# Grouped-query attention in one core: setup order on GpSimd, early transposes, idle matmuls, and the last period's steps

## The chip, the core and the metric

The kernel runs on one core of a Trainium2 chip. The core has five engines that run side by side, each working through its own list of instructions in order: TensorE (PE, matrix products; its weight loads are listed as PEld), VectorE (DVE), ScalarE (ACT), GpSimd (POOL) and SyncE (SP, which here only issues DMAs). They meet by semaphores. Matrix products are written to PSUM, all other tiles lie in SBUF, and DMA queues move data between SBUF and device memory. The metric is the time of one execution on the device in microseconds (us); lower is better. The kernel before takes 414.74 us, the median of three runs (413.86 to 415.82).

## The reference

Softmax attention with 32 query heads and 8 key/value heads, four query heads to each key/value head:

```python
batch, seq, n_heads, n_kv_heads, dim = 8, 512, 32, 8, 64
scale = 1.0 / np.sqrt(dim)
K_expanded = np.repeat(K, heads_per_group, axis=2)
V_expanded = np.repeat(V, heads_per_group, axis=2)
scores = np.einsum('bhqd,bhkd->bhqk', Q, K_expanded) * scale
weights = np.exp(scores - np.max(scores, axis=-1, keepdims=True))
weights = weights / (np.sum(weights, axis=-1, keepdims=True) + 1e-10)
output = np.einsum('bhqk,bhkd->bhqd', weights, V_expanded)
```

Q is (8, 512, 32, 64), K and V are (8, 512, 8, 64), all float32, as is the output.

## The kernel before

**Units, pairs and tiles.** `fast_path` does all the work. (After it a flag says whether every row sum lay in a safe range, and `general_path` would compute everything anew if not; it does not run here.) Two neighbouring key/value heads of one batch with their eight query heads are a *unit*; there are 32 of them (u = 0 to 31). A unit has four *pairs* of query heads. For one pair and one block of 128 keys (kc = 0 to 3), PE writes a *score tile* of 128 keys by 2 x 512 queries (`scores`, L241, two matmuls), and an exponential turns it into a block of weights `pt`. When a pair's four blocks are there, PE multiplies them with V (`pv`, L304, 32 small matmuls in eight *chunks* of four; chunks 6 and 7 belong to the block that comes last). V carries a column of ones, so that the row sums come out beside the result. DVE takes the reciprocal of the sums (`inverse`, L320) and multiplies (`norm`, L331) into the output tile `o_sb` of the unit. `norm` also stores: a unit's 1 MB goes out in one DMA on SP's queue when the fourth of its pairs is done, except in the very last unit (u = 31), where each pair sends its own 256 KB.

**Two ways to take the exponential.** Most score tiles go to ACT (`exp_act`, L255). Of each eight pairs, five have their last block computed elsewhere (`DVE_KCS`): DVE turns the scores into an integer with the bits of a power of two (U, L266), masks them (F, L271), GpSimd computes a correction in two steps (G, L276, and W, L284), and DVE joins both (P, L288).

**The order by hand.** There are 16 *periods* (n = 0 to 15) of eight pairs, two units each. Nothing reorders instructions: each engine's list follows from the order in which the token list is read, `STEPS` for periods up to 14 and `FINISH` for period 15. A token is a letter and a number: S5 fills the sixth ACT score tile of the period, A5 takes its exponential. V5.1-3 does chunks 1 and 2 of pair 5, R5 and N5 its reciprocal and normalisation. D, U, F, G, W, P with a number are the steps of the period's first to fifth DVE exponential, for pairs 0, 1, 3, 5 and 6 (small g and w do the correction on DVE). T transposes a part of Q on PE (with, once, a check of V), C copies it out on DVE, K and H check V, B gathers the check of the sums, Q and k start loads, E ends the check. "@1" means a step of the period before, "@-1" of the next one; "a", "b" and "s" say which PSUM tile is used: `d_ps` (one buffer), `pv` (one) or `s_ps` (two). As `d_ps` and `pv` are single, a step that needs one waits until DVE has read what was in it. With two score tiles, S may fill its tile as soon as ACT is done with the tile before the last.

In period 0 all of pairs 0 and 1 goes through ACT (the A step of a pair's last tile fills and takes the fourth block too), which makes 434 exponentials on ACT.

**The start** (L497 to L530). SP loads Q heads 0 and 1 (`q_start`) and K heads 0 and 1 in two pieces (`k_start`: the first of four 128-key groups, then three). GpSimd makes the identity for PE's transposes, issues loads of Q heads 2 to 3 and 4 to 7 (`load_q(0, (2, 4, 8))`, L505), then sets constants (L506 to L510), then issues the other loads. DMAs that convert float32 to bf16 are issued by GpSimd. PE meanwhile multiplies a tile of zeros (`spin`, L493). The first Q and K parts are cast on DVE and ACT, transposed on PE and copied by DVE.

**Early transposes.** `EARLY` names what PE must still transpose for unit 0 and the first K heads while the first exponentials run: at key 1 the second Q pair of key/value head 0 (four transposes), at 2 the K head 1 (eight), at 3 the Q pairs of head 1 (eight), at 5 and 6 the K heads 2 and 3 (eight each). They stand behind the A step of that number, and each uses `d_ps` and a DVE copy. In period 0, where a V token of the period before has no work, `spin` issues one idle matmul of 256 columns for each of its chunks (L540).

Of the kernel before, what the change touches and what calls it, by code (L numbers as in the profile page):

```python
# [48 lines left out]
).split()  # L49
FINISH = (  # L50
# [10 lines left out]
).split()  # L61


# [19 lines left out]
def fast_path(ctx, tc, Q, K, V, out, flag):  # L83
    nc = tc.nc
    B, S, H, D = Q.shape
# [43 lines left out]
    def load_k(b, lo=0, hi=KV):  # L129
        if b not in kn:  # L130
            kn[b] = knat_pool.tile([128, SC, KV, D], BF16, name="k_nat")
        nc.gpsimd.dma_start(
            out=kn[b][:, :, lo:hi, :],
            in_=K[b, :, lo:hi, :].rearrange("(p sc) g d -> p sc g d", p=128),
        )
# [7 lines left out]
    def load_q(w, cuts=(0, 4 * HPG)):  # L143
        b, half = divmod(2 * w, GP)
        h0 = half * 2 * HPG
        if w not in qn:
            qn[w] = qnat_pool.tile([128, SC, 4 * HPG, D], BF16, name="q_nat")
        for lo, hi in zip(cuts[:-1], cuts[1:]):
            nc.gpsimd.dma_start(  # L149
                out=qn[w][:, :, lo:hi, :],  # L150
                in_=Q[b, :, h0 + lo:h0 + hi, :].rearrange("(sc p) h d -> p sc h d", p=128),
            )

    def d_tile():
        return d_pool.tile([128, 2, S], FP32, name="d_ps")
# [4 lines left out]
    def s_tile():  # L160
        return s_pool.tile([128, 2, S], FP32, name="s_ps")

    def region(tok):
        return {"a": d_tile, "b": pv_tile, "s": s_tile}[tok[-1]]()

    def first_k(gp, g, bank, lo=0, hi=SC):
        half_bank = bank.bitcast(BF16)[:, 0:S]
        ps = half_bank.rearrange("p (sc c) -> p sc c", sc=SC)
        for sc in range(lo, hi):
            for half in (0, 64):  # L170
                nc.tensor.transpose(ps[half:half + 64, sc, :], kn[0][:, sc, 2 * gp + g, :], ident)  # L171
        keys = slice(lo * 128, hi * 128)
        return lambda: nc.vector.tensor_copy(
            out=kt_first[:, gp, g, keys], in_=half_bank[:, keys]
        )
# [11 lines left out]
    def trans_q(u, g, bank, lo=0, hi=NPAIR):  # L187
        ps = bank.bitcast(BF16).rearrange("p (i sc c) -> p i sc c", i=NPAIR, sc=SC)
        for i in range(lo, hi):
            for sc in range(SC):  # L190
                h = ((u % 2) * 2 + g) * HPG + 2 * i
                nc.tensor.transpose(ps[:, i, sc, :], qn[u // 2][:, sc, h:h + 2, :], ident)  # L192
        if u not in qt:
            qt[u] = qt_pool.tile([128, 2, NPAIR, S], BF16, name="qt")
        return lambda: nc.vector.tensor_copy(  # L195
            out=qt[u][:, g, lo:hi, :], in_=ps[:, lo:hi, :, :].rearrange("p i sc c -> p i (sc c)")
        )
# [10 lines left out]
    def early_q(g, lo):  # L208
        return lambda bank: trans_q(0, g, bank, lo)

    def early_k(gp, g):
        return lambda bank: first_k(gp, g, bank)

    EARLY = {1: [early_q(0, 1)], 2: [early_k(0, 1)], 3: [early_q(1, 0)], 5: [early_k(1, 0)],
             6: [early_k(1, 1)]}

    every = [(p, kc) for p in range(PPAIR) for kc in range(SC)]
    ON_DVE = [(p, kc) for p, kc in every if kc in DVE_KCS[p]]
# [2 lines left out]
    def on_dve(n, k):  # L221
        return n * PPAIR + ON_DVE[k][0] >= NPAIR
# [26 lines left out]
    def fill(p, kc):  # L249
        ps = s_tile()  # L250
        scores(p, kc, ps)
        filled[p, kc] = ps

    def exp_act(p, kc):
        nc.scalar.activation(  # L255
            out=pt_of(p)[:, kc, :, :], in_=filled.pop((p, kc)), func=EXP, scale=scale
        )
# [161 lines left out]
    def step(tok, n):  # L419
        what, k = tok[0], int(tok[1:].split(".")[0].rstrip("ab"))  # L420
        q, kc = ON_DVE[k] if what in "DUFGWPgwsa" else (0, 0)
        if what == "S":
            fill(n * PPAIR + ON_ACT[k][0], ON_ACT[k][1])
            if k == 9 and n == 0:
                dma_k(0, TURNED)
            if k == 2 and n % 2 == 1 and n // 2 + 1 < B:
                dma_k(n // 2 + 1)
        elif what == "A":
            q, kc = ON_ACT[k]
            p = n * PPAIR + q  # L430
            exp_act(p, kc)
            if ON_ACT[k + 1:k + 2] == [] or ON_ACT[k + 1][0] != q:
                for d, (dq, dkc) in enumerate(ON_DVE):
                    if dq == q and not on_dve(n, d):
                        fill(p, dkc)
                        exp_act(p, dkc)
            if n == 0 and k in EARLY:
                bank = d_tile()
                for copy in [turn(bank[:, 1, :]) for turn in EARLY[k]]:
                    copy()  # L440
            if (n, k) == (0, 4):
                second_loads()
        elif what in "VRN":
            p = n * PPAIR + k
            if what == "V":
                lo, hi = tok[3:].rstrip("abs").split("-")
                pv(p, int(lo), int(hi), tok)
            else:
                (inverse if what == "R" else norm)(p)
        elif what in "TKCH":  # L450
            j = n * PPAIR // NPAIR + k
            if j < 2:
                pass
            elif what == "T":
                transposes(j, region(tok))
            elif what == "K":
                check_values(j)
            else:
                read(j if what == "C" else (j, "v"))
        elif what == "Q":  # L460
            loads(n, k)
        elif what == "B":
            if n < NPER - 1:
                bulk_check(n)
        elif what == "E":
            (early_check, verdict)[k]()
        elif what in "sa":
            (fill if what == "s" else exp_act)(n * PPAIR + q, kc)
        elif on_dve(n, k):
            p = n * PPAIR + q  # L470
            if what == "D":
                exp_fill(p, kc, region(tok))
                return
            st = chain.get((p, kc))
            if what == "U":
                exp_bits(st)
            elif what == "F":
                exp_low(st)
            elif what in "Gg":
                slope(nc.gpsimd if what == "G" else nc.vector, st["f"], st["g"])  # L480
            elif what in "Ww":
                bend(nc.gpsimd if what == "W" else nc.vector, st["f"], st["g"], st["w"])
            elif what == "P":
                exp_join(p, kc)
# [3 lines left out]
    def spin(count, columns):  # L488
        if not idle:
            idle.append(pv_tile())  # L490
        bank = idle[0]
        for _ in range(count):
            nc.tensor.matmul(  # L493
                bank[:, 1, 0:columns], warm[:, 0:128], warm[:, 0:columns], start=True, stop=True
            )
# [6 lines left out]
            in_=K[0, :, 0:2, :].rearrange("(p sc) g d -> p sc g d", p=128)[:, lo:hi, :, :],  # L502
        )
    make_identity(nc, ident)
    load_q(0, (2, 4, 8))  # L505
    nc.gpsimd.memset(ones, 1.0)  # L506
    nc.gpsimd.memset(off, 0)
    for j in range(2):
        for c in (0, VW - 1):
            nc.gpsimd.memset(vt[j][:, :, :, c:c + 1], 1.0)  # L510
    load_k(0, 2, 4)
    load_q(0, (8, 16))
    load_v(0, 0, 1)
# [15 lines left out]
    copy = first_k(0, 0, s_tile()[:, 0, :], 1, SC)  # L529
    copy()  # L530

    for period in range(-2, NPER):
        for entry in STEPS if period < NPER - 1 else FINISH:
            tok, _, late = entry.partition("@")
            n = period - int(late or 0)
            if 0 <= n < NPER:
                step(tok, n)
            elif period == 0 and n < 0 and tok[0] == "V":
                lo, hi = tok[3:].rstrip("abs").split("-")
                spin(int(hi) - int(lo), S // 2)  # L540


def general_path(tc, Q, K, V, out):
# [114 lines left out]
```

## Time and profile before

| | us |
|---|---|
| median of three runs (lowest, highest) | 414.74 (413.86, 415.82) |
| the profiled execution, its own time | 415.06 |
| span of the profiled execution | 413.2 |
| ACT busy / PE / DVE / POOL | 400.7 / 380.7 / 334.3 / 276.6 |
| first exponential of a score tile starts | 7.75 |
| last exponential ends | 407.83 |

How to read it. The page is of one execution; "busy" is the time an engine worked, and ends of matmuls are modelled. Lines of the timeline give the start, the duration, engine, line of the kernel, operation, output and input, "xN" for N instructions taken together, and in brackets how long the engine was idle before and what ended that. Equal neighbours are merged, so a line's duration can be that of many. "Landing" is the time from the start of a DMA's issue to its completion. Engines overlap the tail of one instruction with the start of the next, so starts are a better measure of the pace than durations.

### The profile page before, as it was taken

How to read it: one execution, taken by the hardware profiler on the slowest of the kernel's cores; microseconds unless marked ns; L12 is line 12 of the kernel's file. 1: busy time of each engine (PE TensorE's matmuls, PEld its weight loads, DVE VectorE, ACT ScalarE, POOL GpSimd, SP SyncE). 2: the span in 40 equal slices, each digit the busy share in tenths (PEclk: the TensorE clock that was granted, in tenths of full speed). 3: DMA queues.
4: the chain of work that ended last, by engine and by line, in shares of the span. 5: the costliest groups of instructions: out<-in, count | busy, mean ns of one | idle time of the engine just before them, and what ended most of it. 6: DMA issues, size and time to landing. Idle time of an engine off the chain costs nothing.

```text
span 413.2 us, 13322 instructions
## 1 busy us (share of the span) xinstructions
PE 380.7 (92%) x5825; PEld 242.1 (59%) x5825; DVE 334.3 (81%) x617; ACT 400.7 (97%) x438; POOL 276.6 (67%) x208
## 2 busy tenths in 40 slices
PE   8999989899998999989899998999989899998995
PEld 3556656566565655656565565656656565665553
DVE  2488897878889788897878889788797878889885
ACT  4999999999999999999999999999999999999994
POOL 8066776677766677676676766667776677766750
PEclk9999999999999999999999999999999999999998
DMA  9969788687769797589865979849788698652205
GB/s 148 197 123 191 190 157 200 156 165 175 158 169 179 129 215 176 138 192 238 170 122 136 181 168 216 202 105 172 194 158 198 165 167 173 158 161 103 103 37 174
DMA packets 65406, 67.74 MB, mean 164 GB/s; under 512 B 35264, under 2 KB 39872, under 8 KB 65344
## 3 DMA queue, kind: packets, MB, share of 16 engines
q0 software_dynamic: 28128, 24.91, 41.1%
q1 hardware_dynamic: 37216, 41.95, 34.4%
q8 instruction: 46, 0.75, 0.7%
q14 instruction: 16, 0.13, 0.1%
HBM read 50.33 MB, written 33.55 MB: 203 GB/s over the span
## 4 chain that ended last, share of the span: by engine, by line
ACT 76%; PE 20%; DMA 1%; DVE 1%; issue 1%; SPq 0%; ACTq 0%
ACT pt L255 76%; PE s_ps L241 9%; PE pv L304 5%; PE d_ps L304 3%; DMA k_start<-in_K_dram 1%; PE pv L493 1%; PE d_ps L192 1%; DVE pt L288 0%; PE d_ps L171 0%; ACTq L255 0%; DVE o_sb L331 0%; PE s_ps L171 0%; ACT k_nat L524 0%; SPq L500 0%; SPq L498 0%
## 5 line engine op out<-in xcount | busy, mean ns | idle before, releaser
L255 ACT ACTIVATE pt<-s_ps 128x1024 f16<-128x1024 f32 x434 | 398.4, 1283 | 2.8 <-PE s_ps L241 2.8
L304 PEld LDWEIGHTS <-pt 128*128 128x128 f16 x4096 | 142.4, 98 | 65.9 <-issue 55.0
L241 PE MATMUL s_ps<-qt,kt 64*128 64x512 bf16 x810 | 158.8, 383 | 23.1 <-ACT pt L255 20.0
L284 POOL TENSOR_TENSOR w<-g,f 128x1024 bf16<-128x1024 bf16 x77 | 164.1, 2132 | 6.4
L276 POOL TENSOR_SCALAR g<-f 128x1024 bf16<-128x1024 int16 x77 | 80.5, 1045 | 115.7 <-DVE f L271 115.7
L304 PE MATMUL pv<-v,pt 128*128 128x65 bf16 x2560 | 114.8, 195 | 0.2
L241 PEld LDWEIGHTS <-kt 64*128 64x128 bf16 x960 | 57.0, 93 | 65.2 <-issue 34.9
L266 DVE TENSOR_SCALAR u<-d_ps 128x1024 int16<-128x1024 f32 x48 | 58.6, 1221 | 19.8 <-PE d_ps L241 19.8
L304 PE MATMUL d_ps<-v,pt 128*128 128x65 bf16 x1536 | 66.6, 194 | 1.2 <-DVE pt L288 0.9
L331 DVE TENSOR_TENSOR o_sb<-pv,inv 128x512 f32<-128x512 f32 x80 | 55.3, 692 | 2.8
L288 DVE TENSOR_TENSOR pt<-u,w 128x1024 uint16<-128x1024 int16 x78 | 54.3, 698 | 2.1 <-POOL w L284 1.1
L192 PEld LDWEIGHTS <-q_nat 128*128 128x128 bf16 x512 | 29.4, 98 | 14.7 <-issue 10.9
L266 DVE TENSOR_SCALAR u<-pv 128x1024 int16<-128x1024 f32 x30 | 36.5, 1216 | 0.0
L195 DVE COPY qt<-d_ps 128x1024 bf16<-128x1024 bf16 (+1 forms) x48 | 32.7, 680 | 3.4 <-PE d_ps L192 3.4
L331 DVE TENSOR_TENSOR o_sb<-d_ps,inv 128x512 f32<-128x512 f32 x48 | 33.2, 691 | 1.6
L271 DVE TENSOR_SCALAR f<-u 128x1024 int16<-128x1024 int16 x78 | 32.7, 419 | 0.1
L192 PE MATMUL d_ps<-ident,q_nat 128*128 128x128 bf16 x380 | 29.8, 222 | 0.0
L320 DVE RECIPROCAL inv<-pv 128x8 f32<-128x8 f32 x80 | 16.5, 206 | 10.5 <-PE pv L304 7.5
L320 DVE RECIPROCAL inv<-d_ps 128x8 f32<-128x8 f32 x48 | 10.0, 208 | 15.6 <-PE d_ps L304 15.1
L241 PE MATMUL d_ps<-qt,kt 64*128 64x512 bf16 x90 | 17.5, 375 | 0.0
L204 DVE TENSOR_REDUCE okv<-d_ps 128x1 f32<-128x128 f32 x31 | 8.9, 287 | 9.3 <-PE d_ps L203 9.3
L149 POOL DMA_DIRECT2D q_nat<-in_Q_dram x18 | 14.7, 815 | 0.2 <-issue 0.2
(49 smaller groups left out, 116.6 us busy)
## 6 DMA issues: line engine op xcount, KB each, us to landing
out_dram<-o_sb SPq DMA_DIRECT2D x31, 1024.0 KB, 5.8
q_nat<-in_Q_dram POOLq DMA_DIRECT2D x15, 1024.0 KB, 9.1
k_nat<-in_K_dram POOLq DMA_DIRECT2D x7, 512.0 KB, 5.2
kt<-kt SPq DMA_DIRECT2D x14, 256.0 KB, 4.4
v<-in_V_dram POOLq DMA_DIRECT2D x7, 512.0 KB, 7.8
out_dram<-o_sb SPq DMA_DIRECT2D x4, 256.0 KB, 2.5
q_nat<-in_Q_dram POOLq DMA_DIRECT2D x1, 512.0 KB, 7.1
v<-in_V_dram POOLq DMA_DIRECT2D x4, 128.0 KB, 7.8
```

What stands on the lines that cost most here:

```text
L192: nc.tensor.transpose(ps[:, i, sc, :], qn[u // 2][:, sc, h:h + 2, :], ident)
L195: return lambda: nc.vector.tensor_copy(out=qt[u][:, g, lo:hi, :], in_=ps[:, lo:hi, :, :].rearrange("p i sc c -> p i (sc c)"))
L241: nc.tensor.matmul(ps[:, m, :], keys[64 * m:64 * m + 64, g if early else g ^ m, kc * 128:(kc + 1) * 128], qt[u][64 * m:64 * m + 64, g, i, ...
L255: nc.scalar.activation(out=pt_of(p)[:, kc, :, :], in_=filled.pop((p, kc)), func=EXP, scale=scale)
L266: nc.vector.tensor_scalar(out=st["u"], in0=st["ps"], scalar1=A_U, scalar2=B_U, op0=ALU.mult, op1=ALU.add)
L271: nc.vector.tensor_single_scalar(out=st["f"], in_=st["u"], scalar=1023, op=ALU.bitwise_and)
L276: engine.tensor_scalar(out=g, in0=f, scalar1=-EXP_F1, scalar2=EXP_K * 2.0 ** (24 * (engine is nc.gpsimd)), op0=ALU.add, op1=ALU.mult,)
L284: engine.tensor_tensor(out=w, in0=g, in1=f, op=ALU.mult)
L288: nc.vector.tensor_tensor(out=pt_of(p)[:, kc, :, :].bitcast(U16), in0=st["u"], in1=st["w"], op=ALU.add)
L304: nc.tensor.matmul(sums[p][:, m, qc, :], pt_of(p)[:, kc, m, qc * 128:(qc + 1) * 128], vt[b % 2][:, kc, gp, g * (D + 1):(g + 1) * (D + 1)], ...
L320: nc.vector.reciprocal(out=invs[n][:, k], in_=sums[p][:, :, :, s:s + 1])
L331: nc.vector.tensor_tensor(out=osb[u][:, :, h:h + 2, :].rearrange("p qc m d -> p m qc d"), in0=sums.pop(p)[:, :, :, o:o + D], in1=invs[p // ...
```

## The change

Four edits:

1. On GpSimd the six memsets of constants come before the two loads of Q heads 2 to 7 instead of behind them.
2. The early transposes stand behind the S step of their number, not behind the A step, and the third of them (the Q pairs of head 1) has number 4 instead of 3.
3. Idle matmuls of period 0 have 128 columns, not 256.
4. `FINISH` has another order. The same steps occur, the same number of chunks, and the three D tiles, U to P, are the same; the sums go in the order of pairs 1, 0, 2, 4, 5, 6, 3, 7 where they went 1, 0, 2, 3, 5, 4, 6, 7. R3 and N3 stand between A25 and A26, P0 and P1 are apart, and pair 7's sum uses a buffer of `s_ps`.

```diff
-    "F1 V5.1-2@1 C1 V5.2-3@1 G1 S1 V5.3-4@1 H1 V5.4-6@1 A0 S2 P4@1 V7.0-1a@1 V5.6-7@1 "
-    "V7.1-2@1 V5.7-8@1 V7.2-3@1 A1 W1 V7.3-4@1 R5@1 S3 N5@1 V7.4-6@1 A2 S4 V6.0-2b@1 "
-    "V7.6-8@1 A3 V6.2-3@1 R7@1 S5 F0 V6.3-5@1 N7@1 V6.5-6@1 G0 A4 S6 V6.6-8@1 D2a A5 R6@1 S7 "
-    "W0 N6@1 U2 A6 S8 T2b A7 S9 C2 V1.0-4a F2 A8 S10 P0 V0.0-2b V1.4-6 P1 A9 S11 V0.2-3 G2 "
-    "V0.3-4 V1.6-8 A10 S12 R1 V0.4-5 N1 V0.5-7 W2 V0.7-8 A11 S13 R0 D3a N0 A12 S14 U3 "
-    "V2.0-4b A13 S15 P2 V2.4-8 A14 F3 S16 R2 T3a G3 N2 K3 A15 S17 V3.0-2b B0@1 V3.2-3 C3 A16 "
-    "W3 S18 V3.3-4 H3 V3.4-7 A17 V3.7-8 S19 R3 D4a N3 A18 S20 U4 V5.0-4b A19 V5.4-5 S21 P3 "
-    "V5.5-6 V4.0-1a A20 S22 F4 V5.6-8 V4.1-3 R5 A21 V4.3-5 N5 S23 V4.5-6 g4 V4.6-7 A22 "
-    "V4.7-8 S24 R4 w4 V6.0-3b A23 V6.3-4 N4 S25 V6.4-6 P4 A24 V7.0-1a S26 E0 V6.6-7 B0@2 "
-    "V6.7-8 V7.1-2 A25 V7.2-3 R6 V7.3-5 N6 V7.5-6 A26 V7.6-8 R7 N7 E1 "
+    "F1 C1 S1 G1 V5.1-3@1 H1 V5.3-6@1 A0 V7.0-1a@1 B0@2 S2 F0 V7.1-2@1 P4@1 V7.2-3@1 A1 S3 "
+    "V5.6-7@1 G0 V7.3-5@1 V5.7-8@1 A2 S4 R5@1 V7.5-6@1 N5@1 V7.6-7@1 W1 V7.7-8@1 A3 S5 R7@1 "
+    "T2b N7@1 A4 S6 C2 D2a U2 W0 A5 S7 V6.0-4b@1 A6 S8 V6.4-5@1 V1.0-1a V6.5-6@1 A7 S9 P1 "
+    "V6.6-7@1 V1.1-4 F2 V1.4-5 A8 V6.7-8@1 S10 R6@1 G2 V1.5-6 N6@1 V1.6-7 A9 S11 V1.7-8 "
+    "V0.0-1b P0 A10 S12 R1 W2 V0.1-3 N1 V0.3-4 A11 S13 D3a V0.4-5 U3 A12 S14 V0.5-8 A13 S15 "
+    "R0 F3 T3a N0 G3 K3 A14 S16 H3 C3 V2.0-3b A15 V2.3-4 W3 S17 D4a V2.4-5 A16 U4 S18 V2.5-8 "
+    "A17 S19 R2 F4 V4.0-3a P3 V4.3-4 A18 S20 N2 V4.4-7 A19 S21 B0@1 V5.0-2b V4.7-8 V5.2-4 "
+    "A20 R4 V5.4-5 g4 S22 N4 V5.5-8 A21 S23 R5 V6.0-1a N5 V6.1-3 A22 S24 w4 V6.3-4 V3.0-2b "
+    "V6.4-5 A23 V3.2-3 P4 S25 V3.3-4 P2 V6.5-7 A24 V6.7-8 S26 R6 V3.4-5 N6 V3.5-7 A25 V3.7-8 "
+    "V7.0-1s E0 V7.1-4 R3 V7.4-6 N3 A26 V7.6-8 R7 N7 E1 "
...
-    EARLY = {1: [early_q(0, 1)], 2: [early_k(0, 1)], 3: [early_q(1, 0)], 5: [early_k(1, 0)],
-             6: [early_k(1, 1)]}
+    EARLY = {1: [early_q(0, 1)], 2: [early_k(0, 1)], 4: [early_q(1, 0)], 5: [early_k(1, 0)], 6: [early_k(1, 1)]}
...
         if what == "S":
             fill(n * PPAIR + ON_ACT[k][0], ON_ACT[k][1])
+            if n == 0 and k in EARLY:
+                bank = d_tile()
+                for copy in [turn(bank[:, 1, :]) for turn in EARLY[k]]:
+                    copy()
...
-            if n == 0 and k in EARLY:
-                bank = d_tile()
-                for copy in [turn(bank[:, 1, :]) for turn in EARLY[k]]:
-                    copy()
...
     make_identity(nc, ident)
-    load_q(0, (2, 4, 8))
     nc.gpsimd.memset(ones, 1.0)
     nc.gpsimd.memset(off, 0)
     for j in range(2):
         for c in (0, VW - 1):
             nc.gpsimd.memset(vt[j][:, :, :, c:c + 1], 1.0)
+    load_q(0, (2, 4, 8))
...
-                spin(int(hi) - int(lo), S // 2)
+                spin(int(hi) - int(lo), S // 4)
```

## The prediction, before the result was known

> **What bounds the kernel now.** I read the page first (engine shares, the chain that ended last, the costliest groups). These three lines are the engines' busy times, the chain by engine, and the costliest group.
>
> ```profile
> PE 380.7 (92%) x5825; PEld 242.1 (59%) x5825; DVE 334.3 (81%) x617; ACT 400.7 (97%) x438; POOL 276.6 (67%) x208
> ...
> ACT 76%; PE 20%; DMA 1%; DVE 1%; issue 1%; SPq 0%; ACTq 0%
> ...
> L255 ACT ACTIVATE pt<-s_ps 128x1024 f16<-128x1024 f32 x434 | 398.4, 1283 | 2.8 <-PE s_ps L241 2.8
> ```
>
> ACT's 434 exponentials take 398.4 of 413.2 us, 0.918 us apiece (1283 ns is one's latency; they overlap). The change leaves their number alone, so only three things can move the time: when the first starts, ACT's 2.8 us of idle before exponentials, and what follows the last. The timeline of ACT over the first 14 us shows the start:
>
> ```profile
> 6.07 0.51 ACT L524 CAST k_nat<-k_start 128x384 bf16<-128x384 f32 x1 [2.04 <-DMA k_start<-in_K_dram]
> 7.75 1.94 ACT L255 ACTIVATE pt<-s_ps 128x1024 f16<-128x1024 f32 x2 [1.17 <-PE s_ps L241]
> 10.21 2.87 ACT L255 ACTIVATE pt<-s_ps 128x1024 f16<-128x1024 f32 x3 [0.52 <-PE s_ps L241]
> ```
>
> The first K tile's DMA lands at 6.04 and starts everything (cast, PE transposes 6.63, scores 7.10, first exponential 7.75). After it ACT idles 0.52 and, at 13.37, 0.29 us. Then it never waits until the last period, whose timeline has the one late wait, behind two joins on DVE:
>
> ```profile
> 390.95 2.13 DVE L288 TENSOR_TENSOR pt<-u,w 128x1024 uint16<-128x1024 int16 x2
> 393.13 0.41 PE L304 MATMUL d_ps<-v,pt 128*128 128x65 bf16 x8 [0.87 <-DVE pt L288]
> 393.48 0.39 PE L241 MATMUL s_ps<-qt,kt 64*128 64x512 bf16 x2
> 393.91 1.02 ACT L255 ACTIVATE pt<-s_ps 128x1024 f16<-128x1024 f32 x1 [0.78 <-PE s_ps L241]
> ```
>
> And the timeline of the end: last weighted sum (its wait is for the last exponential, done at 407.83), last normalisation, last store.
>
> ```profile
> 407.87 0.42 PE L304 MATMUL d_ps<-v,pt 128*128 128x65 bf16 x8 [0.32 <-ACT pt L255]
> 408.94 0.68 DVE L331 TENSOR_TENSOR o_sb<-d_ps,inv 128x512 f32<-128x512 f32 x1
> ```
>
> The last 256 KB store is issued at 409.65 and lands 2.3 us later, 411.95; the span ends 1.25 after that.
>
> **Part 1, constants ahead of the first Q loads.** Nothing is added. On GpSimd the six memsets (3.31 to 3.83, the next issue at 3.60) go ahead of two Q issues that began at 1.61, so these start 0.29 to 0.52 later; every later load is issued when it was. Q heads 2 and 3 landed 4.7 after issue, 6.3, so now about 6.7; they are wanted at 8.16 at the earliest, 7.9 once PE is earlier too. That hides the delay by 1.2 us; without that cover it would cost its 0.29 to 0.52.
> What may be gained: from 3.8 to 5.0 us the DMA queues show 0.13 MB of the hardware queue (K) beside 0.09 MB of the software queue (Q); from 2.4 to 3.4 the hardware queue alone moved 0.26 MB in 1 us. A delay of 0.29 to 0.52 us in which K runs at 0.26 in place of 0.11 MB/us saves it 0.16 to 0.29; a thin tail of 26 packets, 5.0 to 6.04, may shrink as well. No more than 0.67 can come of it: the second K transposes (6.63) stand on PE behind an idle matmul issued at 5.53 that takes until 5.96. Bounds 0 to -0.67; I take **-0.3**, next to the row of the shared stretch.
>
> **Part 2, early transposes behind a score tile, and narrower idle matmuls.** The same transposes and copies, in another order; 256 columns become 128 in idle matmuls of period 0. PE's issue spacing up to 10.1: score pair 0.54, two wide idle matmuls 0.43, four Q transposes 0.43, six K transposes 0.47 (eight: 0.62). Before, score tile 2 started at 7.62 + 0.54 + 0.40 + 0.43 + 0.57 = 9.56 and its exponential 0.65 later, when ACT had been free since 9.69. After: the transposes follow tile 1 and four narrow matmuls take 0.43 in place of 0.83, so it starts near 9.1 and its exponential at 9.75: the 0.52 shrinks to 0.06. But the eight K transposes now stand before the next score tile rather than behind it: 9.1 + 0.54 + 0.62 + 0.21 = 10.5, exponential near 11.1, while ACT is free at 10.67: a new wait of 0.3 to 0.5. Tile 4 now leads its transposes, so the 0.29 goes. What is late next is the tile that follows the second K transposes, as these wait for DVE to copy the eight Q transposes (0.69) out of the only d_ps: by spacing it has 0.1 to spare, so 0 to 0.2. Sum of idle 0.81 before, 0.4 to 0.7 after: I take **-0.3**, bounds -0.8 to +1.0 (the upper end is the cold rival below).
> The clock: Q transposes take 314 ns at 4.72 and 220 at 12.18, a score pair 0.61 at 10.10 less and 0.39 from 10.64 on, though the granted clock reads 1.00 throughout, so PE doubled its pace near 10.4.
> The Trainium skill, "TensorE: Matmul & The Clock Gate", Part 1 (the HAM clock gate), says that PE runs at half rate until a free-running window of about 3.4 us has been busy, and that transposes do not count as other matmuls do. The trace agrees in kind: 3.8 us lie between 6.63, when the last gap ends, and 10.4. By that rule narrower idle matmuls could leave a window short of busy. By the spacings above PE has no gap between 6.63 and 10.5 either way, so I leave the switch where it was.
>
> **Part 3, the last period.** The same steps: 27 exponentials, eight weighted sums, three DVE exponentials, and what is left of period 14. I replayed it with the spacings of the trace: score pair 0.32, chunk of a weighted sum 0.15, eight transposes 0.41, value check 0.24; on DVE the u step 1.22, normalisation 0.60, join 0.59, mask 0.34, reciprocal 0.13 to 0.24. A score tile must start 0.43 before ACT is free.
> The joins P1 and P0 are parted, with the sums that need them behind, so the 0.78 wait goes. The joins ran 1.06 each beside GpSimd's step at 391.12 against 0.68 elsewhere; apart, I allow 0.2 each. Score tiles 10, 17 and 22 then come with 0.15, 0.01 and 0.15 us to spare; late next is tile 17, behind the sum of pair 2 that waits for DVE to finish pair 0's normalisation. Bounds for ACT in this period: -0.78 to +0.6; I take **-0.7**, which brings the last normalisation to about 408.9.
> What does not come free is pair 3. Its normalisation moves from step 18 to between the last two exponentials (about 407.0 to 407.6), and with it the 1 MB store of heads 0 to 7 of this unit, issued at 401.01 before and hidden under 7 us of exponentials. Now it is issued at about 407.6 with pair 7's store behind it on SP's queue. This is what the 401.01 store did, by the rows of the output tensor:
>
> ```profile
> L372 SPq DMA_DIRECT2D out_dram<-o_sb x1: 372/372/372, 401.0 to 401.0; - x1
> ...
> DMA to landing us min/median/max: 6.0/6.0/6.0
> ```
>
> The other 1 MB store of the period (388.5) took 4.1. The 256 KB store issued behind the first, at 404.2, took 3.5 where the others took 2.3 to 2.6: it landed at 407.7, 0.7 after the large one. So the end of stores is 407.6 + (4.1 to 6.0) + 0.7 = 412.4 to 414.3, against 411.95: +0.45 to +2.35, the -0.7 already inside. The rows at 401 (nearest in place) and 388 (alone) have equal claims; I take the middle, **+1.4**.
> The Trainium skill, "DMA: Bandwidth & Descriptors" (Queues, rings and completion order), says that each DMA engine consumes a hardware queue's descriptors in ring order. The 0.7 agrees with it; were the small store free to pass, the end would still be the large one, 0.7 sooner.
>
> **Sum.** -0.3 - 0.3 + 1.4 = +0.8 on the profiled execution: span 413.2 to 414.0, its time 415.06 to 415.9. That execution lies 0.32 above the median of the runs shown (414.74), so the forecast for a median is **415.5**, no change: 0.5% (2.07 us) is about what a measurement of this kernel can tell from none.
>
> **Rivals.**
> A. The late 1 MB store straggles (slower). Mid-kernel stores of this size landed up to 7.4 after issue. Then 407.6 + 7.4 + 0.7 = 415.7, +3.75, less 0.6 at the start: about 417.9. It decides over 0.5% once landing takes more than 6.3. For: 6.0 at 401.01, where a single engine still sent 2 KB packets near 406.5. Against: no loads run at the end. Chance 0.15.
> B. The last period's chains are late: tile 17 or 22 misses by 0.3 to 0.5 twice or thrice, as DVE is the busier for the joins; +1.0 on the sum, 416.5. For: 0.01 to spare. Against: DVE is idle 0.3 to 0.5 in several places. Chance 0.10.
> C. PE stays at half pace for another stretch: four score tiles at +0.22, eight Q transposes +0.43, eight K transposes +0.28, so 1.6, of which ACT's slack takes about half: +0.9, 416.4. Chance 0.07. It is the case that the Trainium skill's rule on the clock would give.
> D. The start gives all it can (K alone -0.67, idle -0.81) and the store is at its short end (+0.45): -1.0, so 413.7. Even this stays within 0.5%. Chance 0.13.
> The forecast itself has 0.55.
>
> **How the numbers follow.** The likeliest case alone spans 414.3 to 416.6 (store 4.1 to 6.0, start by its middle). The range takes in D below and most of A above: 413.2 to 417.6. Slower by over 0.5%: A 0.13, B 0.05, C 0.03, upper end of the forecast 0.03, so 0.24; faster 0.05 (a start better than these bounds, from D); same 0.71.
>
> **What would show it.** The first exponential at about 7.45; idle near 0.06 and 0.4 before the third and fourth; no ACT wait over 0.3 in the last 27; the last normalisation near 408.3 (start gain included); a 1 MB store issued near 407, and the span ending 5 us or more after the last exponential as now, though the arithmetic is done sooner. I am wrong if the last stores land within 2.5 us of the last normalisation, if a wait of over 0.5 us stands before any exponential of the last period, or if half-pace matmuls are found after 11 us.

## The result, and the profile after

The changed kernel takes 417.71 us (median of 6, 416.16 to 418.45) against 414.93 us for the kernel before on the same chip (413.54 to 415.82). The ratio is 1.0069, with a 95% interval of 1.0043 to 1.0095: 2.8 us slower. The profiled execution takes 417.43 us with a span of 415.7, against 415.06 and 413.2 before.

These are the page's lines of the kernel after that answer to those of before (busy times, chain by engine, costliest group), and below them what ACT's exponentials waited for in the last period:

```profile
PE 379.9 (91%) x5825; PEld 243.1 (58%) x5825; DVE 335.2 (81%) x617; ACT 400.7 (96%) x438; POOL 276.3 (66%) x208
...
ACT 73%; PE 21%; DVE 2%; issue 1%; DMA 1%; SPq 0%; ACTq 0%; DVEq 0%
...
L254 ACT ACTIVATE pt<-s_ps 128x1024 f16<-128x1024 f32 x434 | 398.4, 1284 | 3.1 <-PE s_ps L240 3.1
```

```profile
ACT pt L254 <- PE s_ps L240: 2.4, 3, 1.4
```

ACT's work is the same 398.4 us. Its total of waits is little different (3.1 in place of 2.8), but they have moved: 2.4 us now stand in the last period, where 0.78 stood. The timeline of ACT shows the start, which is clean, and the three late waits:

```profile
6.22 0.51 ACT L523 CAST k_nat<-k_start 128x384 bf16<-128x384 f32 x1 [1.93 <-DMA k_start<-in_K_dram]
7.50 13.06 ACT L254 ACTIVATE pt<-s_ps 128x1024 f16<-128x1024 f32 x14 [0.77 <-PE s_ps L240]
...
395.06 1.02 ACT L254 ACTIVATE pt<-s_ps 128x1024 f16<-128x1024 f32 x1 [1.41 <-PE s_ps L240]
396.38 1.02 ACT L254 ACTIVATE pt<-s_ps 128x1024 f16<-128x1024 f32 x1 [0.29 <-PE s_ps L240]
398.06 10.19 ACT L254 ACTIVATE pt<-s_ps 128x1024 f16<-128x1024 f32 x11 [0.66 <-PE s_ps L240]
```

Ahead of the waits, the timeline of DVE, GpSimd and PE has the cause. In time order: GpSimd's multiply for pair 3 (W2), the join of pair 0 (P0), and the scores of D3, which wait for the normalisation behind that join:

```profile
390.19 2.13 POOL L283 TENSOR_TENSOR w<-g,f 128x1024 bf16<-128x1024 bf16 x1
390.32 2.54 DVE L287 TENSOR_TENSOR pt<-u,w 128x1024 uint16<-128x1024 int16 x1
...
393.01 0.69 DVE L330 TENSOR_TENSOR o_sb<-d_ps,inv 128x512 f32<-128x512 f32 x1
393.76 0.39 PE L240 MATMUL d_ps<-qt,kt 64*128 64x512 bf16 x2 [1.49 <-DVE o_sb L330]
```

A free join takes 0.68. This one took 2.54 and ended at 392.86, 0.54 after GpSimd's multiply (392.32). The windows of the changed kernel show what followed on PE (columns: stretch, its length, then busy time of PE, PEld, DVE, ACT and POOL with instructions, granted PE clock, DMA share, GB/s):

```profile
392.30:393.70 1.40, 0.00 (x0) 0.00 (x0) 1.37 (x3) 1.35 (x2) 0.01 (x1) 1.00 1.01 379
394.40:397.40 3.00, 3.00 (x29) 2.03 (x28) 2.11 (x4) 2.05 (x2) 0.98 (x1) 0.50 0.02 5
```

PE stood still for 1.49 us (1.4 of it in the first stretch), and soon after it resumed its clock fell to 0.50. The second stretch shows 3 us of that; by the trace's records of the granted clock it lasted from 394.11 to 397.52. The waits of 0.29 and 0.66 lie in or just behind that slow stretch.

The last piece is the end: the rows of the output tensor for the last store of the changed kernel (issue, then time to landing).

```profile
L371 SPq DMA_DIRECT2D out_dram<-o_sb x1: 372/372/372, 410.1 to 410.1; - x1
...
DMA to landing us min/median/max: 4.5/4.5/4.5
```

From the last exponential to the last store's issue it is 1.85 us (408.25 to 410.1), about as before (407.83 to 409.65). The store then lands after 4.5 in place of 2.3.

The difference of the two spans therefore comes to: first exponential 7.50 in place of 7.75, -0.25; idle of ACT behind it, none in place of 0.81; waits in the last period 2.36 in place of 0.78, +1.58; last store +2.2. The sum is +2.7, where the spans differ by 2.5.

### The profile page after: what moved, and what is told of

The parts are those of the page before. It is cut to its first block, busy times and chain, and to the rows that moved or that the text cites. A ratio compares the mean times of both kernels' runs of the same rounds, so it can differ in the third digit from the quotient of the medians.

```text
span 415.7 us, 13321 instructions
## 1 busy us (share of the span) xinstructions
PE 379.9 (91%) x5825; PEld 243.1 (58%) x5825; DVE 335.2 (81%) x617; ACT 400.7 (96%) x438; POOL 276.3 (66%) x208
## 4 chain that ended last, share of the span: by engine, by line
ACT 73%; PE 21%; DVE 2%; issue 1%; DMA 1%; SPq 0%; ACTq 0%; DVEq 0%
ACT pt L254 73%; PE s_ps L240 10%; PE pv L303 6%; PE d_ps L303 4%; DMA k_start<-in_K_dram 1%; DVE o_sb L330 1%; PE d_ps L192 1%; DVE pt L287 0%; DVE inv L319 0%; ACTq L254 0%; DVE w L283 0%; PE d_ps L240 0%; PE pv L192 0%; ACT k_nat L523 0%; SPq L499 0%
## 5 line engine op out<-in xcount | busy, mean ns | idle before, releaser
L254 ACT ACTIVATE pt<-s_ps 128x1024 f16<-128x1024 f32 x434 | 398.4, 1284 | 3.1 <-PE s_ps L240 3.1
L287 DVE TENSOR_TENSOR pt<-u,w 128x1024 uint16<-128x1024 int16 x78 | 55.4, 711 | 2.1 <-POOL w L283 2.0
```

The costliest lines, as they stand in the source:

```text
L254: nc.scalar.activation(out=pt_of(p)[:, kc, :, :], in_=filled.pop((p, kc)), func=EXP, scale=scale)
L287: nc.vector.tensor_tensor(out=pt_of(p)[:, kc, :, :].bitcast(U16), in0=st["u"], in1=st["w"], op=ALU.add)
```

## The experiments

All kernels compute the whole result. Each time is a median beside runs of the kernel before on the same chip; ratios are to those.

**The new start with the old last period.** Only `FINISH` goes back.

```diff
-FINISH: F1 C1 S1 G1 V5.1-3@1 ... (the new list)
+FINISH: F1 V5.1-2@1 C1 V5.2-3@1 G1 S1 ... (the old list)
```

> The start of the changed kernel (parts 1 and 2) with the last period of the kernel before. Theory: the start is a gain in itself (first exponential at 7.5 in place of 7.75 and almost no idle of ACT after it), so the first 17 us give 0.6 to 1.1 us and the last period is as in the kernel before: ACT waits once there, about 0.8, and the last store lands 2.3 after its issue. Time 413.8 to 414.5, that is 0.1 to 0.3% below the kernel before. Rival (the start costs something that the profile hides, such as PE at half pace for longer): ACT idles 0.8 or more in the first 17 us and the time is 415 or more.

Measured: 414.48 us, ratio 0.9983 (0.9963 to 1.0003). The last period is that of the kernel before to the digit: one wait of 0.78 and a last landing 2.3 after issue. In the first 17 us this execution did idle, 0.31 and 0.42. The sum of 0.73 lies between the two expectations, while the time is the theory's. PE had been at full pace early, waited 1.51 us for K, and then ran at half pace until about 11.2 us, which the rival had named. The timeline of PE and the windows (columns as above, the granted clock third from the end) show it:

```profile
6.96 0.36 PE L171 MATMUL s_ps<-ident,k_nat 128*64 128x128 bf16 x6 [1.51 <-ACT k_nat L523]
```

```profile
8.00:9.00 1.00, 1.00 (x9) 0.69 (x8) 0.04 (x1) 1.00 (x2) 0.62 (x1) 0.50 1.15 178
9.00:10.00 1.00, 1.00 (x10) 0.37 (x9) 0.39 (x1) 0.69 (x2) 0.26 (x2) 0.50 1.20 197
```

The start is not the same in every execution; more on that below.

**The new last period with the old start.**

```diff
-FINISH: F1 V5.1-2@1 C1 V5.2-3@1 G1 S1 ... (the old list)
+FINISH: F1 C1 S1 G1 V5.1-3@1 ... (the new list)
```

> The kernel before with the new last period alone. Theory: all of the loss is in the last period, so this is slower than the changed kernel by what the start gave, 0.6 to 1.1: time 418.2 to 418.8, with ACT's waits at 2 to 2.6 us in the last period and the last store landing 4 us or more after its issue. Rival (the parts act on one another, for instance the join meets GpSimd's multiply only because the start shifted the clocks): the waits differ from the changed kernel's by over 0.5 and the time is under 417.5.

Measured: 417.88 us, ratio 1.0078 (1.0052 to 1.0104). The loss is in the last period. Its join is again held, 2.53 us, and ended 0.56 after GpSimd's multiply, by the timelines of GpSimd and DVE:

```profile
390.57 2.12 POOL L284 TENSOR_TENSOR w<-g,f 128x1024 bf16<-128x1024 bf16 x1
...
390.72 2.53 DVE L288 TENSOR_TENSOR pt<-u,w 128x1024 uint16<-128x1024 int16 x1
```

ACT waited 2.0 there (1.08 and 0.91), and the last landing was 4.6 after issue. The meeting of join and multiply is not an accident of the new start. The time is 0.3 under the expected 418.2: with the old start, too, this profile has no idle of ACT behind the first exponential.

**Clear of GpSimd.** The changed kernel with the mask F2, and so G2 and W2 behind it, after the join P0.

```diff
-... V1.1-4 F2 V1.4-5 A8 V6.7-8@1 S10 R6@1 G2 V1.5-6 ... V0.0-1b P0 A10 ...
+... V1.1-4 V1.4-5 A8 V6.7-8@1 S10 R6@1 V1.5-6 ... V0.0-1b P0 F2 G2 A10 ...
```

> The changed kernel with F2 and G2 (mask and first GpSimd step of pair 3) moved behind P0, so that no GpSimd step is running when P0, the join of pair 0, starts. Theory: the join at 390.32 took 2.54 us because GpSimd's multiply (390.19 to 392.32) had begun 0.13 before it and held it until its end; clear of it the join takes 0.68, PE never idles 1.5 us, its clock stays at 1.00, and ACT's three waits in the last period (1.41, 0.29, 0.66) go: none over 0.3. Span about 2.2 shorter than the changed kernel's 415.7, time 415.2 to 415.6. Rival (the join waits for its own data or for the order on DVE): the join stays over 2 us and the waits stay at 2 us or more.

Measured: 414.91 us, ratio 1.0004 (0.9987 to 1.0021) where the changed kernel had 1.0069, and 0.3 under the expected 415.2; the span is 413.2. The timelines of DVE and GpSimd, and then of ACT, of this run:

```profile
390.07 0.68 DVE L287 TENSOR_TENSOR pt<-u,w 128x1024 uint16<-128x1024 int16 x1
390.67 0.42 DVE L270 TENSOR_SCALAR f<-u 128x1024 int16<-128x1024 int16 x1
...
392.30 2.12 POOL L283 TENSOR_TENSOR w<-g,f 128x1024 bf16<-128x1024 bf16 x1
...
393.68 1.03 DVE L270 TENSOR_SCALAR f<-u 128x1024 int16<-128x1024 int16 x1
```

```profile
396.39 9.27 ACT L254 ACTIVATE pt<-s_ps 128x1024 f16<-128x1024 f32 x10 [0.24 <-PE s_ps L240]
```

The join takes 0.68, PE's clock stays at 1.00 in every microsecond from 390 to 397, and 2.36 us of waits become 0.24. The rival is out. The late store stays: the last landing is 4.6 after its issue. Also to be seen: the moved multiply now meets the next mask, which takes 1.03 in place of 0.42 and ends 0.29 after the multiply; that is what the 0.24 comes from.

**Small stores.** The changed kernel with unit 30 stored pair by pair.

```diff
-        if u == NU - 1:
+        if u >= NU - 2:
             store(u, h, h + 2)
```

> The changed kernel with unit 30 stored pair by pair as unit 31 is (four DMAs of 256 KB in place of one of 1 MB). Theory: the last store of the changed kernel landed 4.5 us after its issue because 1 MB issued 1.2 us earlier stood ahead of it; with 256 KB there it lands 2.3 to 3.1 after, and the span is 1.4 to 2.2 shorter, time 415.4 to 416.2; ACT's waits in the last period stay at about 2.4. Rival (something else sets the end, or small stores disturb more): the last landing stays at 4 us or more after its issue, or the time stays within 0.5 of 417.7.

Measured: 415.56 us, ratio 1.0018 (1.0002 to 1.0033). The rows of the output tensor for its last store:

```profile
L371 SPq DMA_DIRECT2D out_dram<-o_sb x1: 372/372/372, 410.9 to 410.9; - x1
...
DMA to landing us min/median/max: 2.3/2.3/2.3
```

It lands 2.3 after its issue, and the span is 414.6 though the arithmetic of this execution ended later (last issue 410.9, not 410.1). ACT's waits in the last period stay: 2.3.

**Both repairs.** The last two edits together.

```diff
-... V1.1-4 F2 V1.4-5 ... R6@1 G2 V1.5-6 ... V0.0-1b P0 A10 ...
+... V1.1-4 V1.4-5 ... R6@1 V1.5-6 ... V0.0-1b P0 F2 G2 A10 ...
-        if u == NU - 1:
+        if u >= NU - 2:
```

> The changed kernel with both repairs: F2 and G2 behind P0, and unit 30 stored pair by pair. Theory: the two losses of the changed kernel add up and are all there is; clear of the held join its arithmetic ended at 407.6 (410.2 in the changed kernel), and with small stores the last lands 2.3 to 2.8 after its issue. Span 411 to 411.8, time 412.7 to 413.6, 0.4 to 0.6% below the kernel before. Rival (the end is not set by the store but by something at a fixed time after the arithmetic, or the repairs overlap): 414 or more.

Measured: 413.33 us, ratio 0.9960 (0.9942 to 0.9977), span 411.6; the join 0.68, one wait of 0.24 in the last period, last landings 2.3 to 2.8. The two losses account for the whole: by ratios the edits gave 0.65% and 0.51% alone and 1.09% together. The changed kernel so mended is faster than both kernels.

**The same hold in the kernel before.** There two joins in a row, from 390.95 on, took 2.13, and GpSimd's step began 0.17 after the first, as the timeline of GpSimd before shows:

```profile
391.12 1.41 POOL L276 TENSOR_SCALAR g<-f 128x1024 bf16<-128x1024 int16 x1 [1.30 <-DVE f L271]
```

The mask that released that step moves behind both.

```diff
-... S9 C2 V1.0-4a F2 A8 S10 P0 V0.0-2b V1.4-6 P1 A9 ...
+... S9 C2 V1.0-4a A8 S10 P0 V0.0-2b V1.4-6 P1 F2 A9 ...
```

> The kernel before with one token moved: F2 (mask of pair 3) behind P1. Its two joins at 390.95 took 2.13 us, the second held until GpSimd's step at 391.12 ended. Theory: with the mask behind the joins GpSimd starts after them, each takes 0.68, and ACT's one wait in the last period (0.78) goes; time 0.6 to 0.8 below the kernel before, that is 0.15 to 0.2%. Rival (the joins are slow for another reason): they still take 2.0 or more and the wait stays.

Measured: 414.45 us, ratio 0.9975 (0.9962 to 0.9988). The timelines of DVE and ACT of this run:

```profile
389.35 1.28 DVE L288 TENSOR_TENSOR pt<-u,w 128x1024 uint16<-128x1024 int16 x2
390.55 0.42 DVE L271 TENSOR_SCALAR f<-u 128x1024 int16<-128x1024 int16 x1
```

```profile
7.38 398.28 ACT L255 ACTIVATE pt<-s_ps 128x1024 f16<-128x1024 f32 x434 [0.78 <-PE s_ps L241]
```

Two joins take 1.28, and all 434 exponentials run without a gap (that none stands at the start either is not the token's doing). One token, moved, is worth 0.25% (interval 0.12 to 0.38); the 0.78 us of the wait alone would be 0.19%. The 0.78 wait that the new `FINISH` was to be rid of was this hold, and not the neighbourhood of the two joins.

**The new start with that last period.** The changed kernel with the old `FINISH`, so mended.

```diff
-FINISH: F1 C1 S1 G1 V5.1-3@1 ... (the new list)
+FINISH: F1 V5.1-2@1 C1 ... V1.0-4a A8 S10 P0 V0.0-2b V1.4-6 P1 F2 A9 ... (the old list, F2 behind P1)
```

> The new start with the last period of the kernel before, in which F2 stands behind P1. It has the early 1 MB store and no held join. Theory: the start's 0.3 to 0.7 and the held join's 0.7 add up: span near 412, time 413.4 to 414.0, 0.25 to 0.45% below the kernel before and 0.3 to 0.8 us slower than the run with both repairs. Rival: the old last period hits another wait once the held join is gone, and the time is not under 414.3.

Measured: 413.60 us, ratio 0.9950 (0.9931 to 0.9969), a time inside the expected 413.4 to 414.0. The 0.3 to 0.8 us that it was to be behind the run with both repairs did not show: that one had 0.9960, and the two can't be told apart. So no run shows the new `FINISH` to be better than the old one, once both are mended.

**What the start is worth.** Both repairs with the old start, that is the kernel before with the new `FINISH` and both edits:

```diff
-    EARLY = {1: ..., 2: ..., 4: ..., 5: ..., 6: ...}   (behind S; idle matmuls of S // 4)
+    EARLY = {1: ..., 2: ..., 3: ..., 5: ..., 6: ...}   (behind A; idle matmuls of S // 2)
     make_identity(nc, ident)
+    load_q(0, (2, 4, 8))
     nc.gpsimd.memset(ones, 1.0)
...
-    load_q(0, (2, 4, 8))
     load_k(0, 2, 4)
```

> As the run with both repairs, but with the start of the kernel before (GpSimd's Q loads first, early transposes behind the exponential, wide idle matmuls). It prices the new start against it on one chip. Theory: the new start is worth 0.4 to 0.8 us, so this is that much slower: 413.2 to 414.2. Rival (the new start is worth nothing measurable, the time of the first exponential being set by the K DMA and by the moment at which PE doubles its pace): within 0.3 us of the run with both repairs.

Measured: 415.15 us, ratio 0.9987 (0.9964 to 1.0010). That is neither expectation. Its times fall in two groups, five of 412.8 to 413.7 and seven of 415.0 to 416.7, so the median says little; the profile was of the lower group. Two more profiles of the same kernel:

> The run with both repairs and the old start once more, for a profile: its times lay in two groups, 412.8 to 413.7 and 415.0 to 416.7. Theory: in the upper group PE doubles its pace only after 10 us, and the old order of transposes and wide idle matmuls then costs ACT 0.8 us or more of idle before 17 us, where the new one costs 0.3 to 0.7; in the lower group PE doubles by 7.5 and ACT has no idle after its first exponential. Rival (the two groups differ elsewhere, for instance in the last period): the first 17 us look alike in both.

> The same kernel as the run before it, one more profile, with the same expectations: idle of ACT of 0.8 us or more before 17 us in an execution of the upper group by the theory, and none that differs there by the rival.

One fell into each group: 413.33 and 416.32 us. Their timelines of ACT at the start, first of the lower and then of the upper:

```profile
6.26 0.51 ACT L524 CAST k_nat<-k_start 128x384 bf16<-128x384 f32 x1 [2.22 <-DMA k_start<-in_K_dram]
7.55 389.06 ACT L255 ACTIVATE pt<-s_ps 128x1024 f16<-128x1024 f32 x424 [0.78 <-PE s_ps L241]
```

```profile
7.03 0.51 ACT L524 CAST k_nat<-k_start 128x384 bf16<-128x384 f32 x1 [2.94 <-DMA k_start<-in_K_dram]
8.70 1.94 ACT L255 ACTIVATE pt<-s_ps 128x1024 f16<-128x1024 f32 x2 [1.16 <-PE s_ps L241]
11.16 2.10 ACT L255 ACTIVATE pt<-s_ps 128x1024 f16<-128x1024 f32 x2 [0.52 <-PE s_ps L241]
13.90 1.02 ACT L255 ACTIVATE pt<-s_ps 128x1024 f16<-128x1024 f32 x1 [0.63 <-PE s_ps L241]
15.21 384.34 ACT L255 ACTIVATE pt<-s_ps 128x1024 f16<-128x1024 f32 x419 [0.29 <-PE s_ps L241]
```

The last periods are alike (0.24 of wait in both). The start differs by 2.6 us: K 0.77 later, the first exponential 1.67 after the cast began in place of 1.29, and 1.44 of idle behind it. In the slow one a pair of score matmuls took 0.61 until 13.25 and 0.39 from 14.78 on; in the fast one it was 0.39 from 8.73 at the latest. In these two profiles, one of each group, the theory holds and the rival falls.

**The GpSimd order alone undone,** with both repairs and the rest of the new start.

```diff
     make_identity(nc, ident)
+    load_q(0, (2, 4, 8))
     nc.gpsimd.memset(ones, 1.0)
...
-    load_q(0, (2, 4, 8))
     load_k(0, 2, 4)
```

> Both repairs, the new early transposes and narrow idle matmuls, but GpSimd's Q loads ahead of its constants as in the kernel before: part 1 alone is undone. The casts of the second K piece began at 5.96 to 6.95 with the new order and at 6.07 to 6.66 with the old one, so part 1 has shown nothing so far. Theory: part 1 is worth nothing, the time is that of the run with both repairs, 413.0 to 413.7, and the K cast begins between 5.9 and 7.0. Rival (part 1 carries the start's gain by an earlier K): 414.5 or more, with the cast later than 6.7.

Measured: 414.11 us, ratio 0.9985 (0.9970 to 1.0000); the cast began at 6.86. The time lies between the two expectations. By ratios this is 0.25% above the run with both repairs, but on another chip, and the intervals meet. The second K cast began at 5.96 to 6.95 in six profiles with the new order (mean 6.30) and at 6.07 to 7.03 in seven with the old (mean 6.49): a difference of 0.2 inside a spread of 1 us. Whether part 1 does anything stays open.

## Why the prediction was wrong

The forecast was 415.5 and "no change", the range 413.2 to 417.6; measured were 417.71 and a loss clear of noise. What failed is the price of the joins in part 3; by steps:

**Part 1, constants first (-0.3): not shown.** K's cast began at 6.22 in the changed kernel, later than the 6.07 before. No run confirms the value taken. The first exponential came at 7.50, close to the 7.45 that the prediction named, but this was luck: not an earlier K brought it, but PE at full pace, with 1.28 from the cast to the exponential in place of 1.68.

**Part 2, early transposes and idle matmuls (-0.3): right in kind, and its worth depends on the execution.** "I leave the switch where it was" was the weak step, as the start has three forms.
- PE was at full pace before 7.5 us and stayed there, in three of seven profiles with the new order of transposes and four of six with the old. Then ACT had no idle behind its first exponential, whichever order it was.
- PE doubled its pace only between 10 and 14 us, in three profiles. The old order then idled 0.81 and 1.44. The new one, in the run with small stores, idled 0.31 before the fourth exponential, where the prediction had worked out 0.3 to 0.5.
- PE was at full pace early, waited 1.51 to 1.90 us for K, and went back to half pace from about 8 to 11.5 us, in three profiles, all with the new order (one of them with GpSimd's old order). ACT idled 0.42 to 0.73.

The old order was not met in the third form, and no run shows whether the edits have a part in which form comes. The profiled execution of before was of the second form and that of after of the first, so its -1.06 is more than the edit's.

**Part 3, the joins ("apart, I allow 0.2 each", and so -0.7): this failed.** It was the wait for P0, 1.86 us over a free join, that made +1.58 of -0.7, an error of 2.3 us. I had the right row in hand, 1.06 each at 390.95 beside GpSimd's step, and read it as two joins slowed evenly. The rows of that line tell more than the mean: the longest of all 78 joins took 1.525 us, and it is one of these two, so one was nearly free and one was held until GpSimd's step ended. A price that is "until the other is done" can be 0 or 2 us, and no average of it is a bound; I gave it none from above beyond +0.6. The sign that I had named, a wait of over 0.5 before an exponential of the last period, is what the trace shows.

**The clock in the last period: not foreseen.** A gap of 1.49 us on PE was followed by 3.4 us of half pace. I put the 0.29 and 0.66 on top of the first wait down to it; no run parts the slow clock from the held join, and both go when the join is clear. Rival C had a slow clock at the start only, though half pace after 11 us was among the signs that the prediction had named.

**The late 1 MB store (+2.1 beside the -0.7): right.** It landed 4.2 after its issue, the last store 4.5 after its own, +2.2. With small stores it was 2.3. Rival A, a straggling store, did not occur, and that its 417.9 is near the measured 417.71 is chance; the short end of 4.1 was the nearer row, and the wait behind it 1.5 in place of 0.7 (413.1 to 414.6).

**Rival B** (chains of the last period late) named the right place and sign with the wrong tile and a price of +1.0.

**A slip in the sums.** The likeliest case's span of 414.3 to 416.6 does not come out of its terms: 0.45 to 2.35 with the -0.6 of the start gives 414.6 to 416.5. Nothing else hangs on it.

## What to carry to other kernels

Where DVE and GpSimd both work on SBUF tiles, look for each DVE operation with all its tiles in SBUF that starts while a GpSimd operation runs, and price it as "waits until that one ends", not by a mean slowdown; in a hand-written order, hold the release of the GpSimd step back until the DVE operation has begun. A large store that is moved past the last exponentials lengthens the end, here by 2.2 us, by way of the small store queued behind it. A wait on PE is worth more than its length if it is long enough to bring its clock down.

## What the runs showed of the hardware

**DVE held by GpSimd.** In each of the two profiles of before and after, two joins began while GpSimd worked on a step of its own. All four end 0.54 to 0.55 after GpSimd's operation, however much of it was left; a free join takes 0.68. One mask in each began 0.08 before GpSimd's end and took 0.43, as a free one does (0.42). A mask was held in the run with F2 moved: 1.03, ending 0.29 after the multiply. Joins that began while GpSimd was issuing a load were not held (0.68 at 98.58 of the changed kernel, within an issue of 1.23). Nor were steps that read PSUM: beside the two multiplies at 383.88 to 388.09 of the changed kernel a normalisation took 0.69, a copy 0.69 and a u step 1.22, as elsewhere. The other way round GpSimd's step gets longer: 1.42 in place of 1.04 when a join had begun just before it. The Trainium skill, "Advanced Engine Details and Errata" (GPSIMD Details), says that GpSimd shares a read and a write interface with DVE and conflicts with DVE instructions in a two-port mode or with two SBUF inputs; that section gives no size. A join has two inputs in SBUF, and the runs agree and show the size: the rest of the other's operation, here up to 2 us.

**PE's clock after a short gap.** Three executions with the held join had a PE gap of 1.49 to 1.50 us, and in each the granted clock fell to 0.50 within 2 us of its end: at 394.11, 395.25 and 396.47, where the gaps had ended at 393.76, 394.15 and 394.56. It was back 3.41 later each time (at 397.52 in the changed kernel). The three executions with a wait of 1.51 to 1.90 for K at the start lost the clock for 3.41 us as well. The gap of 0.87 in the kernel before, and gaps of up to 1.08 at the start of other runs with the clock up, did not bring it down. The Trainium skill, "TensorE: Matmul & The Clock Gate" (Why this matters for your kernels), warns of gaps over about 3 us; here half of that was enough. That the window is free-running, as the same page says (Part 1), fits the times: within an execution the changes of the clock lie whole multiples of 3.41 us apart (394.11, 397.52 and 411.18 in the changed kernel), and not at a fixed distance from the gap.

**The start's clock.** In the three executions in which PE ran at half pace until some moment between 10 and 14 us, the kernel before among them, the granted clock was given as 1.00 all the while, so that there only the durations of the matmuls tell. The half pace that came back at about 8 us in the other three it does give, as 0.50.
